# The down projection of two SwiGLU blocks in Strassen's seven block products

## The chip, the cores and the metric

The kernel runs on one core of a Trainium2 chip. The metric is the device time of one execution in microseconds (us). TensorE (PE) multiplies, VectorE (DVE) and ScalarE (ACT) work on tiles in the two on-chip memories SBUF and PSUM, GpSimd (POOL) works on SBUF tiles, and DMA queues bring weights from HBM; most transfers are issued by SyncE (SP).

## The reference

Two layers of a decoder trunk over 512 positions of width 1024, in float32. Each layer mixes tokens with four groups of heads, projects out, and then runs a SwiGLU block of inner width 2816:

```python
for l in range(DEPTH):                      # DEPTH = 2
    h = rms_norm(x, norm_mix_w[l])
    ...                                     # in projection, four token mixers
    x = x + y @ w_out[l]
    h = rms_norm(x, norm_ffn_w[l])
    x = x + (silu(h @ w_gate[l]) * (h @ w_up[l])) @ w_down[l]
return rms_norm(x, final_norm_w)
```

The change is in the last product of a layer, by `w_down` (2816 x 1024).

## The kernel before

**Layout.** Activations lie transposed: `x[0..7]` are eight tiles of 128 channels x 512 positions. The inner width 2816 makes KF = 22 tiles `j` of 128 rows ("hidden tiles"), the output width KD = 8 tiles `m`.

**Precision.** Every matmul operand is split into a high part (a copy to fp32r by ACT) and a low part (value minus high part, by DVE or POOL). `mm3` issues three matmuls for one 128x128 weight block: high x high, high x low, low x high (lines L429, L430, L431). The weights are split on the fly: `split_w` (L249, L250) for plain pieces, `s_item` (L341 to L359) for Strassen pieces.

**Order.** `items` is a list, written out ahead, of weight pieces in the order in which PE uses them. `w_next` takes the next one, splits one or more later ones ahead (up to AHEAD = 5 Strassen items) and lets SP load later pieces (L323). Split weights lie in four slots of the pool `wsp`, and within the SwiGLU part in four more of `ffw`. PSUM is two pools of four banks each, `pd` and `pm`. The framework orders the instructions of each engine by program order and a simulated time line, so that work that is ready may go ahead of work that is not.

**The SwiGLU part of a layer.** For the first five hidden tiles (`hidden_plain`, N_PLAIN = 5) gate and up are plain products: 8 blocks x 3 matmuls of 512 columns each. Meanwhile `operand(k)`, k = 0..3, prepares the seven Strassen operands of the normalised x: DVE and ACT build e, g, h, t1, t2, t3, t4 (each 256 columns wide; L1487 to L1495) in `bh`, `bl`. From tile 5 on, `hidden(j)` computes gate and up together as a 2x2 block product with seven block products instead of eight (`product`, 4 blocks x 3 matmuls of 256 columns each, so 84 matmuls a step). The two weight pieces of a step give seven items: a, b, d as they are, and s1, s2, s4 (sums made by DVE in a `pd` bank) and s3 (made by POOL). The seventh product and the multiplication of a step (L1556) are put off into the next step by `last` and `finish`. `leave_hidden` then splits the finished tile (ACT L1504, DVE L1505).

**The down projection** is plain, in two parts, because the split tiles don't all fit: `SPLIT_FF = [15, 7]` gives layer 0 a first part of 15 hidden tiles and a second of 7, layer 1 a first of 7 and a second of 15. `down(part)` runs for each `m` over the tiles of its part, 3 matmuls of 512 columns each, into a `pd` bank, and adds the sum to `x[m]` (L1587). In the second part of layer 0 `x[m]` is also split for the next layer and stored by SP (L1594). In the second part of layer 1 the last two `m` are done in two halves of 256 columns (`down_order`, TAIL = 2); within the second run of the first of these second halves `leave(0)` scales the finished first half (`rstd_spread`, DVE and POOL L1568 and L1566) and issues its stores from SP and ACT (L1569). `leave(1)` does the same for the second half at the end.

Of the kernel before, what the change touches and what calls it, by code (L numbers as in the profile page):

```python
# [16 lines left out]
P = 128  # L17
# [22 lines left out]
SPLIT_FF = [15, 7]  # L40
# [90 lines left out]
def kernel(  # L131
# [135 lines left out]
    def ff_parts(l):  # L267
        return [range(0, SPLIT_FF[l]), range(SPLIT_FF[l], KF)]

    def part_order(l, part):  # L270
        return down_order(l) if part else [(m, slice(0, T)) for m in range(KD)]

    def eights(ks, short=False):

        n = 4 if short else 0
        return [ks[:n]] * short + [ks[i:i + 8] for i in range(n, len(ks), 8)]

    for l in range(DEPTH):
        for nm in ORDER:
            if nm == "gg":  # L280
                for g in range(2):
                    plain(wg[l, g], 4 * (G + 2 * H))
            elif nm in T_GROUPS:
                for g in range(2):
                    plain(wt[l, 2 * T_GROUPS.index(nm) + g], 4 * G)
            else:
                plain(wc[l, C_TILES.index(nm)], KD * P)
        for m, g in OUT_ORDER:
            plain(wo[l, m][:, g * 4 * P:(g + 1) * 4 * P], 4 * P)
        left = None  # L290
        for part, js in enumerate(ff_parts(l)):
            for j in js:
                if j < N_PLAIN:
                    for q in range(2):
                        plain(wf[l, 2 * j + q], KD * P, V)
                    continue
                pj = len(pieces)
                pieces.extend((wf[l, 2 * j + q], KD * P) for q in range(2))
                for u in ("a", "s1", "d", "s2", "b", "s4", "s3"):
                    if u != "d":  # L300
                        items.append((u, pj))
                    elif left is not None:
                        items.append((u, left))
                left = pj
            for n_m, (m, _) in enumerate(part_order(l, part)):
                for n8, k8 in enumerate(eights(js, n_m == 0)):
                    plain(wd[l, m][:, k8[0] * P:(k8[-1] + 1) * P], len(k8) * P)
                    if n_m == n8 == 0 and left is not None:
                        items.append(("d", left))
                        left = None  # L310
# [1109 lines left out]
    for l in range(DEPTH):  # L1420
# [47 lines left out]
        with tc.tile_pool(name=f"ffp{l}", bufs=1, reuse_waits="tile") as ffp, \  # L1468
# [3 lines left out]
            own = [[ffp.tile([P, T], F32R, name=f"{q}{k}") for q in ("ph", "pl")] for k in range(KF - max(SPLIT_FF))]  # L1472
            both_h = own + [[xh[k], xl[k]] for k in range(KD)]
            hid = {j: both_h[n] for js in ff_parts(l) for n, j in enumerate(js)}

            HC = T // 2
            bh = [ffp.tile([P, 7 * HC], F32R, name=f"bh{k}") for k in range(KD // 2)]
            bl = [ffp.tile([P, 7 * HC], F32R, name=f"bl{k}") for k in range(KD // 2)]
            B_E, B_G, B_H, B_T1, B_T2, B_T3, B_T4 = (slice(n * HC, (n + 1) * HC) for n in range(7))

            def operand(k):
                ef, gh = fft.tile([P, T], F32, name="gs"), fft.tile([P, T], F32, name="sg")
                t12, t34 = pm.tile([P, T], F32, name="pm"), pm.tile([P, T], F32, name="pm")
                lo, up = slice(0, HC), slice(HC, T)
                for q, t in enumerate((ef, gh)):
                    kk = k + q * KD // 2
                    V.scalar_tensor_tensor(t, x[kk], col(o + V_NFFN + kk), rsb, op0=MUL, op1=MUL)  # L1487
                V.tensor_tensor(t12[:, lo], ef[:, up], ef[:, lo], op=SUB)
                V.tensor_tensor(t34[:, lo], ef[:, up], gh[:, up], op=ADD)
                V.tensor_tensor(t12[:, up], gh[:, up], t12[:, lo], op=ADD)  # L1490
                V.tensor_tensor(t34[:, up], gh[:, lo], t12[:, up], op=SUB)
                for t, c in ((ef[:, lo], B_E), (gh, slice(HC, 3 * HC)), (t12, slice(3 * HC, 5 * HC)),
                             (t34, slice(5 * HC, 7 * HC))):
                    S.copy(bh[k][:, c], t)  # L1494
                    V.tensor_tensor(bl[k][:, c], t, bh[k][:, c].bitcast(F32), op=SUB)  # L1495

            def product(ps, c, first=False):
                hi, lo = w_next()
                for k in range(KD // 2):
                    mm3(ps, hi, lo, k, bh[k][:, c], bl[k][:, c], first and k == 0, k == KD // 2 - 1, True)  # L1500

            def leave_hidden(j, v):
                hi, lo = hid[j]
                S.copy(hi, v)  # L1504
                V.tensor_tensor(lo, v, hi.bitcast(F32), op=SUB)  # L1505

            def hidden_plain(j):
# [7 lines left out]
                gs = fft.tile([P, T], F32, name="gs")  # L1515
                sg = fft.tile([P, T], F32, name="sg")
                V.tensor_tensor(gs, pg, rsb, op=MUL)
                S.activation(sg, gs, AF.Silu)
                V.tensor_tensor(sg, sg, rsb, op=MUL)
                V.tensor_tensor(gs, pu, sg, op=MUL)  # L1520
                leave_hidden(j, gs)
# [9 lines left out]
            def hidden(j):  # L1531
# [13 lines left out]
                S.copy(gs[:, up], cd[:, lo])
                product(ab[:, lo], B_G)
                product(ab[:, up], B_H)
                V.tensor_tensor(ab, ab, gs, op=ADD)
                S.activation(sg, ab, AF.Silu)
                product(cd[:, lo], B_T3)  # L1550
                S.copy(u3, cd[:, lo])
                V.tensor_tensor(cd[:, up], cd[:, up], u3, op=ADD)

                def end():
                    product(cd[:, lo], B_T4)
                    V.tensor_tensor(cd, cd, sg, op=MUL)  # L1556
                    leave_hidden(j, cd)
                last.append(end)

# [11 lines left out]
            def down(part):  # L1571
                js = ff_parts(l)[part]
                order = part_order(l, part)
                for n_m, (m, c) in enumerate(order):
                    ps = pd.tile([P, T], F32, name="pd")[:, c]
                    for n8, k8 in enumerate(eights(js, n_m == 0)):
                        hv = w_next()
                        for n, k in enumerate(k8):
                            ph, pl = hid[k]
                            mm3(ps, *hv[n // 4], n % 4, ph[:, c], pl[:, c], k == js[0], k == js[-1])  # L1580
# [6 lines left out]
                    V.tensor_tensor(x[m][:, c], x[m][:, c], ps, op=ADD)  # L1587
                    if not part:
                        continue
# [8 lines left out]
                return sq if part and l + 1 == DEPTH else None  # L1598

            for part, js in enumerate(ff_parts(l)):  # L1600
                for j in js:
# [3 lines left out]
                sq = down(part)  # L1605
# [6 lines left out]
def pack(inputs):  # L1612
# [55 lines left out]
    wd = np.stack([np.stack([ctile(a["ffn_w_down"][l][:, m * P:(m + 1) * P]) for m in range(KD)])  # L1668
# [25 lines left out]
```

## Time and profile before

| what | value |
|---|---|
| median of 3 runs | 1355.92 us (1354.26 to 1356.53) |
| the profiled execution | 1356.95 us, its span 1355.1 us |
| PE busy, its weight loads busy | 1308.9 us (97%), 1166.0 us (86%) |
| DVE, ACT, POOL busy | 752.9 (56%), 647.9 (48%), 737.1 us (54%) |
| mean granted PE clock | 0.975 |
| HBM read and written | 117.61 and 6.82 MB |

The profile follows one execution. A line such as L1587 is a line of the kernel. In a row of a group, "out<-in" gives the tiles by name, then their shapes, the count, the busy time and the mean duration; what stands behind "idle before" is how long the engine had waited just before and for whom. [...] The two SwiGLU parts lie at about 328 to 681 us and 990 to 1344 us.

### The profile page before, as it was taken

The page shows a single profiled execution, that of the slowest core. Times are in us where ns is not written, and L with a number is a line of the kernel's source. Part 1 is how long each engine was busy: PE and PEld are TensorE (multiplying, and loading weights), DVE is VectorE, ACT ScalarE, POOL GpSimd, SP SyncE. Part 2 cuts the span into 40 slices and gives each one's busy share as a digit, 9 for nine tenths or more (in the row PEclk, how much of TensorE's full clock was granted, in tenths as well). Part 3 has the DMA queues.
Part 4 walks back from the last instruction along what each step waited for, and adds up shares of the span by engine and source line. Part 5 has one row for each costly group of instructions (what it writes and reads, how often), then busy time and mean ns, then how long its engine had stood idle before and what let it go on. Part 6 is the DMA issues. An engine that isn't in the chain of part 4 may idle for free.

```text
span 1355.1 us, 22065 instructions
## 1 busy us (share of the span) xinstructions
PE 1308.9 (97%) x8402; PEld 1166.0 (86%) x8402; DVE 752.9 (56%) x1305; ACT 647.9 (48%) x1276; POOL 737.1 (54%) x627
## 2 busy tenths in 40 slices
PE   8899988999999999999999999999999999999997
PEld 6788987988889988899888887888887889999887
DVE  4653769637886620255456367777569336655113
ACT  5453454535556632365445345445444436666333
POOL 5376674933046644565545766747602366666444
PEclk8899989989999999999999999989999999999998
DMA  6223210134223333233432222002422333233333
GB/s 245 66 77 105 65 48 9 48 93 129 89 84 110 109 99 101 91 100 111 149 110 94 80 80 73 23 5 75 142 92 85 88 104 113 96 109 113 95 96 112
DMA packets 58506, 125.85 MB, mean 93 GB/s; under 512 B 17312, under 2 KB 24736, under 8 KB 58400
## 3 DMA queue, kind: packets, MB, share of 16 engines
q1 hardware_dynamic: 56960, 123.27, 28.9%
q8 instruction: 66, 1.08, 0.3%
q10 hardware_dynamic: 1440, 1.18, 0.3%
q14 instruction: 40, 0.33, 0.1%
HBM read 117.61 MB, written 6.82 MB: 92 GB/s over the span
## 4 chain that ended last, share of the span: by engine, by line
PE 86%; DVE 7%; POOL 3%; ACT 1%; issue 1%; DMA 1%; POOLq 0%; SPq 0%; DVEq 0%; ACTq 0%
PE pd L429 15%; PE pd L430 15%; PE pd L431 15%; PE pm L429 8%; PE pm L430 8%; PE pm L431 8%; PE pd L459 2%; PE pd L458 2%; PE pd L457 2%; PE pm L1126 2%; POOL wlo L250 1%; DVE x L1229 1%; PE pm L865 1%; POOL ar L718 0%; PE pm L1019 0%
## 5 line engine op out<-in xcount | busy, mean ns | idle before, releaser
L250 POOL TENSOR_TENSOR wlo<-wraw,whi 128x512 fp32r<-128x512 f32 (+1 forms) x240 | 309.1, 1295 | 260.5 <-ACT whi L249 258.9
L249 ACT CAST whi<-wraw 128x512 fp32r<-128x512 f32 (+2 forms) x288 | 173.5, 606 | 329.0 <-PE pd L430 232.1
L430 PE MATMUL pm<-bl,whi 128*128 128x256 f32 x952 | 267.5, 282 | 3.5 <-DVE bl L1495 3.5
L429 PE MATMUL pm<-bh,whi 128*128 128x256 f32 x952 | 267.4, 283 | 1.8 <-ACT bh L1494 1.0
L359 POOL TENSOR_TENSOR wlo<-wraw,whi 128x512 fp32r<-128x512 f32 x136 | 179.0, 1328 | 158.6 <-ACT whi L358 142.2
L431 PE MATMUL pm<-bh,wlo 128*128 128x256 f32 x952 | 265.0, 281 | 0.0
L429 PE MATMUL pd<-xh,whi 128*128 128x512 f32 (+1 forms) x592 | 232.6, 394 | 4.8 <-DVE pm L914 2.3
L430 PE MATMUL pd<-xl,whi 128*128 128x512 f32 (+1 forms) x592 | 231.6, 392 | 1.0 <-DVE xl L244 1.0
L431 PE MATMUL pd<-xh,wlo 128*128 128x512 f32 (+1 forms) x592 | 231.2, 392 | 0.0
L430 PEld LDWEIGHTS pm<-bl,whi 128*128 128x128 f32 x952 | 181.1, 190 | 4.4 <-DVE bl L1495 3.9
L429 PEld LDWEIGHTS pm<-bh,whi 128*128 128x128 f32 x952 | 180.7, 190 | 4.5 <-PE pd L431 1.6
L431 PEld LDWEIGHTS pm<-bh,wlo 128*128 128x128 f32 x952 | 180.0, 190 | 0.1
L429 PEld LDWEIGHTS pd<-xh,whi 128*128 128x128 f32 x592 | 112.7, 190 | 29.5 <-ACT ar L1029 2.4
L430 PEld LDWEIGHTS pd<-xl,whi 128*128 128x128 f32 x592 | 112.5, 190 | 25.7 <-DVE xl L244 2.8
L431 PEld LDWEIGHTS pd<-xh,wlo 128*128 128x128 f32 x592 | 112.7, 190 | 24.0
L358 ACT CAST whi<-wraw 128x512 fp32r<-128x512 f32 x136 | 84.5, 622 | 53.3 <-PE pm L430 29.1
L457 PE MATMUL pd<-whi,xh 128*128 128x256 f32 (+1 forms) x320 | 93.5, 294 | 5.5 <-DVE ar L562 4.4
L458 PE MATMUL pd<-wlo,xh 128*128 128x256 f32 (+1 forms) x320 | 93.8, 294 | 0.0
L459 PE MATMUL pd<-whi,xl 128*128 128x256 f32 (+1 forms) x320 | 93.2, 293 | 0.0
L430 PE MATMUL pd<-pl,whi 128*128 128x512 f32 (+1 forms) x238 | 90.4, 381 | 0.0
L429 PE MATMUL pd<-ph,whi 128*128 128x512 f32 (+1 forms) x238 | 90.3, 382 | 0.0
L1587 DVE TENSOR_TENSOR x<-x,pd 128x512 f32<-128x512 f32 (+1 forms) x34 | 22.0, 655 | 123.0 <-PE pd L431 123.0
(317 smaller groups left out, 2521.2 us busy)
## 6 DMA issues: line engine op xcount, KB each, us to landing
wraw<-in_wf_dram SPq DMA_DIRECT2D x88, 512.0 KB, 3.5
wraw<-in_wc_dram SPq DMA_DIRECT2D x35, 512.0 KB, 3.5
wraw<-in_wd_dram SPq DMA_DIRECT2D x30, 448.0 KB, 3.3
wraw<-in_wd_dram SPq DMA_DIRECT2D x18, 512.0 KB, 3.6
wraw<-in_wt_dram SPq DMA_DIRECT2D x16, 512.0 KB, 3.5
wraw<-in_wo_dram SPq DMA_DIRECT2D x32, 256.0 KB, 2.6
x<-in_xt_dram SPq DMA_DIRECT2D x16, 256.0 KB, 4.3
wraw<-in_wg_dram SPq DMA_DIRECT2D x4, 528.0 KB, 3.6
```

The costliest lines, as they stand in the source:

```text
L249: S.copy(hi[:, :n], r)
L250: eng.tensor_tensor(lo[:, :n], r, hi[:, :n].bitcast(F32), op=SUB)
L358: S.copy(hi, src)
L359: eng.tensor_tensor(lo, src, hi.bitcast(F32), op=SUB)
L429: PE.matmul(ps, hi[:, w], ah, start=first, stop=False, skip_group_check=shared)
L430: PE.matmul(ps, hi[:, w], al, start=False, stop=False, skip_group_check=shared)
L431: PE.matmul(ps, lo[:, w], ah, start=False, stop=last, skip_group_check=shared)
L457: PE.matmul(o, xh[k][:, tk], hi[:, w], start=(k == 0 and b % per == 0), stop=False)
L458: PE.matmul(o, xh[k][:, tk], lo[:, w], start=False, stop=False)
L459: PE.matmul(o, xl[k][:, tk], hi[:, w], start=False, stop=(k == KD - 1 and b % per == per - 1))
L1126: PE.matmul(ps[:, (bb * 2 + ct) * P:(bb * 2 + ct + 1) * P], k[:, ct * T + b * P:ct * T + (b + 1) * P], qx[:, (ct * NB + b) * P:(ct * NB + ...
L1587: V.tensor_tensor(x[m][:, c], x[m][:, c], ps, op=ADD)
```

## The change

The down projection of hidden tiles 0 to 7 (part 0) and 8 to 15 (part 1) is also done by Strassen's seven products, two output tiles `m = 2q, 2q+1` at a time, so four steps of 84 matmuls a part; tiles 16 to 21 (`rest`) stay plain. Part 0 runs after hidden tile 8, part 1 after hidden tile 16. The body of `hidden(j)` becomes `step(of, first, second)`, used by both. A finished hidden tile is no longer split as it is: it goes to a `sqp` tile, and the seven operands of a pair of tiles are built by `blocks_even` and `blocks_odd` in banks of `pm` (tiles below 5) or `pd`. The same two functions replace the body of `operand`. `leave(0)` moves from within item (6, second half) to after the matmuls of (7, second half). The rows of `w_down` are packed in another order.

```diff
+PART = 8
+N_PARTS = KF // PART
...
+    steps = []
+    for j in range(KF):
+        steps.append(("hidden", j))
+        if j and j % PART == 0:
+            steps += [("down", j // PART - 1, q) for q in range(KD // 2)]
+    steps.append(("rest",))
+    rest = range(PART * N_PARTS, KF)
...
+                two = [wd[l, m][:, part * PART * P:(part + 1) * PART * P] for m in (2 * q, 2 * q + 1)]
...
-                late = i >= len(items) - 4 * TAIL
+                late = i >= len(items) - 2 * TAIL
...
+            own = [ffp.tile([P, T], F32R, name=f"ph{k}") for k in range(2 * 7)]
+            seven = own + xh + xl
+            seven = [seven[7 * k:7 * k + 7] for k in range(PART // 2)]
+            hid = {j: own[2 * n:2 * n + 2] for n, j in enumerate(rest)}
...
+            def split(v, hi, lo):
+                S.copy(hi, v)
+                V.tensor_tensor(lo, v, hi.bitcast(F32), op=SUB)
...
+            def blocks_even(pool, ef, of):
+                t1 = bank(pool)
+                V.tensor_tensor(t1[:, LO], ef[:, UP], ef[:, LO], op=SUB)
+                split(ef[:, LO], *of("e"))
+                split(t1[:, LO], *of("t1"))
+
+            def blocks_odd(pool, ef, gh, of, gh_, t23_):
+                t23, t4 = bank(pool), bank(pool)
+                V.tensor_tensor(t23[:, UP], ef[:, UP], gh[:, UP], op=ADD)
+                V.tensor_tensor(t23[:, LO], t23[:, UP], ef[:, LO], op=SUB)
+                V.tensor_tensor(t4[:, LO], gh[:, LO], t23[:, LO], op=SUB)
+                split(gh, *gh_)
+                split(t23, *t23_)
+                split(t4[:, LO], *of("t4"))
...
+            def hidden_split(j):
+                if j in rest:
+                    split(raw.pop(j), *hid[j])
+                    return
+                pool, k = pm if j < N_PLAIN else pd, j % PART // 2
+                if j % 2 == 0:
+                    blocks_even(pool, raw[j], lambda nm: of_hidden(k, nm))
+                else:
+                    blocks_odd(pool, raw.pop(j - 1), raw.pop(j), lambda nm: of_hidden(k, nm), seven[k][3:5], seven[k][5:7])
...
+                def up(cd):
+                    if j in rest and j != rest[0]:
+                        raw[j] = cd
+                        V.tensor_tensor(cd, cd, sg, op=MUL)
+                        hidden_split(j)
+                    else:
+                        raw[j] = sqp.tile([P, T], F32, name="sq")
+                        V.tensor_tensor(raw[j], cd, sg, op=MUL)
+                        if j % PART or j == 0:
+                            hidden_split(j)
+                step(of_x, lambda ab: S.activation(sg, ab, AF.Silu), up)
+
+            def down(part, q):
+                def add(m):
+                    return lambda ps: V.tensor_tensor(x[m], x[m], ps, op=ADD)
+                step(of_hidden, add(2 * q), add(2 * q + 1))
+                if q == KD // 2 - 1:
+                    last.append(lambda: hidden_split(PART * (part + 1)))
...
-                        if part and l + 1 == DEPTH and n_m == KD:
-                            if n8 == 0:
-                                rstd_sum(range(NB // 2), ssq)
-                            else:
-                                leave(0)
+                    if l + 1 == DEPTH and n_m == KD:
+                        rstd_sum(range(NB // 2), ssq)
+                    if l + 1 == DEPTH and n_m == KD + 1:
+                        leave(0)
                     V.tensor_tensor(x[m][:, c], x[m][:, c], ps, op=ADD)
```

More of the change, by code (lines that the diff above doesn't have):

```diff
@@ L39 @@
 N_PLAIN = 5
-SPLIT_FF = [15, 7]
+PART = 8
+N_PARTS = KF // PART
+DOWN_K = [PART * p + k for p in range(N_PARTS) for k in (*range(0, PART, 2), *range(1, PART, 2))] + list(
+    range(PART * N_PARTS, KF))
 AHEAD = 5
@@ L265, in plain, with runs @@
         pieces.append((ap, n))
[L267 to L276, printed above, removed]
+    steps = []
[5 more added lines that the diff above has]
+    rest = range(PART * N_PARTS, KF)
+    def runs(short=False):
+        return [rest[:4], rest[4:]] if short else [rest]
     for l in range(DEPTH):
@@ L290 @@
         left = None
[L291 to L295, printed above, removed]
-                    continue
[L297 to L310, printed above, removed]
+        for what, *n in steps:
+            if what == "rest":
+                for n_m, (m, _) in enumerate(down_order(l)):
+                    for r in runs(n_m == 0):
+                        plain(wd[l, m][:, r[0] * P:(r[-1] + 1) * P], len(r) * P)
+                        if left is not None:
+                            items.append(("d", left))
+                            left = None
+                continue
+            if what == "hidden":
+                two = [wf[l, 2 * n[0] + q] for q in range(2)]
+                if n[0] < N_PLAIN:
+                    for ap in two:
+                        plain(ap, KD * P, V)
+                    continue
+            else:
+                part, q = n
+                two = [wd[l, m][:, part * PART * P:(part + 1) * PART * P] for m in (2 * q, 2 * q + 1)]
+            pj = len(pieces)
+            pieces.extend((ap, KD * P) for ap in two)
+            for u in ("a", "s1", "d", "s2", "b", "s4", "s3"):
+                if u != "d":
+                    items.append((u, pj))
+                elif left is not None:
+                    items.append((u, left))
+            left = pj
     raws, halves, sums = {}, {}, {}
@@ L1497, in product @@
[L1497 to L1505, printed above, removed]
+                    if q == 0:
+                        blocks_even(pm, t, lambda nm: of_x(k, nm))
+                blocks_odd(pm, *two, lambda nm: of_x(k, nm), *([t[:, n * HC:(n + 2) * HC] for t in bx[k]] for n in (1, 4)))
@@ L1529, in finish, with step, product @@
                 last.clear()
-            def hidden(j):
+            def step(of, first, second):
+                def product(ps, nm, start=False):
+                    hi, lo = w_next()
+                    for k in range(KD // 2):
+                        mm3(ps, hi, lo, k, *of(k, nm), start and k == 0, k == KD // 2 - 1, True)
                 ab = pm.tile([P, T], F32, name="pm")
@@ L1546, in hidden @@
[L1546 to L1557, printed above, removed]
@@ new lines, in step, with end, hidden @@
+                first(ab)
+                product(cd[:, LO], "t3")
+                S.copy(u3, cd[:, LO])
+                V.tensor_tensor(cd[:, UP], cd[:, UP], u3, op=ADD)
+                def end():
+                    product(cd[:, LO], "t4")
+                    second(cd)
+                last.append(end)
+            def hidden(j):
+                sg = fft.tile([P, T], F32, name="sg")
+                def up(cd):
[3 more added lines that the diff above has]
+                        hidden_split(j)
+                    else:
+                        raw[j] = sqp.tile([P, T], F32, name="sq")
+                        V.tensor_tensor(raw[j], cd, sg, op=MUL)
+                        if j % PART or j == 0:
+                            hidden_split(j)
+                step(of_x, lambda ab: S.activation(sg, ab, AF.Silu), up)
@@ L1604 @@
                         operand(j)
-                sq = down(part)
+                elif what == "down":
+                    down(*n)
+                else:
+                    sq = down_rest()
             extra.clear()
```

87 lines of the change are left out of this document (42 added, 45 removed).

## The prediction

> **What bounds the kernel now.** I read the page's busy shares first, then its chain of waits, then the stages by windows.
>
> ```profile
> PE 1308.9 (97%) x8402; PEld 1166.0 (86%) x8402; DVE 752.9 (56%) x1305; ACT 647.9 (48%) x1276; POOL 737.1 (54%) x627
> PE 86%; DVE 7%; POOL 3%; ACT 1%; issue 1%; DMA 1%; POOLq 0%; SPq 0%; DVEq 0%; ACTq 0%
> ```
>
> PE is busy 97% of the span and holds 86% of the chain, so fewer or shorter matmuls pay where PE stays fed. What a matmul costs is its pace, read in stretches bounded by an instruction that comes once a step (L1556) or once an output tile (L1587).
>
> ```profile
> core 0: us, PE busy (x) PEld busy (x) DVE busy (x) ACT busy (x) POOL busy (x), PEclk, DMA share, GB/s
> 1143.10:1252.90 109.80, 109.76 (x928) 109.16 (x927) 66.42 (x108) 69.06 (x142) 71.11 (x55) 1.00 0.33 107
> 412.88:482.22 69.34, 69.34 (x588) 69.03 (x588) 42.99 (x69) 43.73 (x91) 44.99 (x35) 1.00 0.32 100
> 596.09:635.32 39.23, 39.23 (x333) 39.04 (x332) 23.41 (x39) 24.97 (x52) 26.28 (x22) 1.00 0.30 95
> L1556 DVE TENSOR_TENSOR pm<-pm,sg x12: 699/700/700, 1143.1 to 1252.9; 128x512 f32<-128x512 f32 x12
> L1587 DVE TENSOR_TENSOR x<-x,pd x7: 686/689/689, 509.8 to 572.5; 128x512 f32<-128x512 f32 x7
> L1587 DVE TENSOR_TENSOR x<-x,pd x4: 686/688/689, 1280.3 to 1311.6; 128x512 f32<-128x512 f32 x4
> 1321.78:1343.99 22.21, 22.21 (x189) 1.00 0.29 87
> ```
>
> The first three windows hold 11, 7 and 4 Strassen steps (12 L1556 bound 11), together 218.4 us for 22 steps: 9.92 us a step, 0.1181 us for each of 84 matmuls of 256 columns. Plain: 6 output tiles of 45 matmuls in 62.7 us are 0.2324 us each in layer 0, 3 in 31.3 us are 0.2313 us in layer 1. The plain half-width tail takes 22.2 us for 180 matmuls and 8 tiny ones; allowing some 0.7 us for those, 0.119 us. PE is never idle there: PE busy equals the window.
>
> [...]
>
> **The matmuls.** Layer 0 loses 384 plain ones (16 tiles x 8 x 3) and gains 672 (8 steps x 84): 89.2 - 79.4 = 9.8 us. Layer 1 loses 330 of full width (438 become 108) and 108 of half width (180 become 72, as the halved tail runs over 6 tiles instead of 15), and gains 672: 76.3 + 12.9 - 79.4 = 9.8 us. Sum **-19.6 us**.
>
> **VectorE in the steps.** A finished pair of tiles costs 7 operations of 256 columns and 2 of 512 instead of 2 of 512.
>
> ```profile
> L1505 DVE TENSOR_TENSOR pl<-pm,ph 128x512 fp32r<-128x512 f32 x7 | 4.8, 690 | 2.9 <-ACT ph L1504 2.9
> L1552 DVE TENSOR_TENSOR pm<-pm,u 128x256 f32<-128x256 f32 x15 | 6.4, 429 | 6.8 <-ACT u L1551 6.8
> L341 DVE TENSOR_TENSOR pd<-wraw 128x512 f32<-128x512 f32 x13 | 10.3, 790 | 10.9 <-DMA wraw<-in_wf_dram 10.9
> L345 DVE TENSOR_TENSOR pd<-wraw,pd 128x512 f32<-128x512 f32 x14 | 9.6, 685 | 0.0
> L359 POOL TENSOR_TENSOR wlo<-wraw,whi 128x512 fp32r<-128x512 f32 x56 | 72.8, 1313 | 33.2 <-ACT whi L358 29.9 <-PE pm L430 1.9 <-PE pm L431 0.4
> L1545 ACT COPY gs<-pm 128x256 f32<-128x256 f32 x15 | 5.6, 375 | 0.0
> L1504 ACT CAST ph<-pm 128x512 fp32r<-128x512 f32 x7 | 4.1, 588 | 4.7 <-DVE pm L1556 4.7
> ```
>
> With 0.43 and 0.69 us that is +0.6 us for an even tile, +2.4 for an odd one (3 + 1 of 256, 2 of 512, less one). DVE has 66.42/11 = 6.0 us in a step of 9.9, so 6.6 and 8.4. ACT rises from 6.3 by at most 1.0 (copies of 0.59 + 0.59 + 0.38 less 0.59); POOL stays at 6.5. Down steps have DVE at 6.0 too (two additions to `x` for the multiplication and the split). All fit in 9.9, so on average the cover holds, but an odd step leaves DVE 1.5 us. I take 1 us in all for late operands in the 22 steps with tiles 5 to 15; bounds 0 (today PE doesn't wait) and 8.
>
> How the upper bound comes: four new operations of a pair have both inputs in SBUF. L341 has that form and takes 0.79 us where L345, with one input in PSUM, takes 0.69. The worst that such an operation shows is this row, beside POOL's work:
>
> ```profile
> 385.75 1.79 DVE L1505 TENSOR_TENSOR pl<-gs,ph 128x512 fp32r<-128x512 f32 x1
> ```
>
> That is 1.1 us over the 0.69. With two of those an odd step takes DVE 10.6 us, 0.7 too long: 8 us over the 12 odd steps (5 to 15, two layers) if even steps (8.8) take up none of it. [...]
>
> **VectorE between plain tiles and Strassen steps.** This is the one place where DVE is the bound already.
>
> ```profile
> 344.88:393.83 48.95, 46.30 (x211) 38.26 (x210) 48.52 (x80) 26.87 (x50) 12.75 (x8) 0.97 0.23 76
> 387.46 0.42 DVE L1491 TENSOR_TENSOR pm<-sg,pm 128x256 f32<-128x256 f32 x1
> 387.79 1.44 DVE L1519 TENSOR_TENSOR sg<-sg,rsb 128x512 f32<-128x512 f32 x1
> 389.33 0.69 DVE L1520 TENSOR_TENSOR gs<-pd,sg 128x512 f32<-128x512 f32 x1
> 389.94 1.28 DVE L1495 TENSOR_TENSOR bl<-pm,bh 128x512 fp32r<-128x512 f32 x2
> 388.55 0.39 PE L429 MATMUL pm<-bh,whi 128*128 128x256 f32 x1 [0.46 <-ACT bh L1494]
> 390.68 0.58 PE L430 MATMUL pm<-bl,whi 128*128 128x256 f32 x1 [1.74 <-DVE bl L1495]
> 393.62 0.41 PE L431 MATMUL pm<-bh,wlo 128*128 128x256 f32 x1
> 393.83 0.34 PE L429 MATMUL pm<-bh,whi 128*128 128x256 f32 x1
> 1052.47 0.38 PE L430 MATMUL pm<-bl,whi 128*128 128x256 f32 x1 [1.74 <-DVE bl L1495]
> ```
>
> DVE works 48.5 of 48.95 us, and PE waits 0.46 + 1.74 us for the last operand of x. Then its matmuls start 0.21 us apart for some 3 us instead of 0.118: another 1.3 us, at a granted clock of 0.97 in the stretch. So 3.5 us a layer are lost today (layer 1 shows the same 1.74). Back to back, a DVE operation costs 0.33 us (387.46 to 387.79) or 0.61 (389.33 to 389.94). Splitting tiles 0 to 3 adds 7 of 0.33 for each pair, 4.7 us for both, ahead of the last operand. Against it, `blocks_even` delivers e and t1 before anything else, where today t1 shares a copy with t2; the 24 matmuls of e and t1 and those of t2, g and h on k = 0..2 give some 3 us before PE needs the rest. What is late next is then t2 of k = 3. Bounds a layer: -3.5 (the wait goes) to +4.7 (all of it shows). `operand` now holds three `pm` banks instead of two, and the tile splits one or two of the same four, so I stay above the middle (+0.6): **+1.5 us a layer, +3 in all**.
>
> **The end.** Today `leave(0)` hides beside matmuls of (7, second half):
>
> ```profile
> 1340.36 0.39 PE L234 MATMUL pm<-cs,rst 128*128 128x128 f32 x2
> 1341.41 1.75 DVE L1568 TENSOR_TENSOR x<-x,pm 128x256 f32<-128x256 f32 x5 [1.11 <-ACT rsb L238]
> 1341.46 2.14 POOL L1566 TENSOR_TENSOR x<-x,rsb 128x256 f32<-128x256 f32 x3 [1.44 <-ACT rsb L238]
> 1341.87 1.90 ACTq L1569 DMA_DIRECT2D out_dram<-x  x4
> 1343.88 0.28 PE L431 MATMUL pd<-xh,wlo 128*128 128x256 f32 x1
> 1344.65 0.42 ACT L213 ACTIVATE sq<-x 128x256 f32<-128x256 f32 x1 [3.26 <-DVE x L1587]
> 1346.00 0.70 POOL L205 TENSOR_TENSOR rst<-ms,mhalf 128x2 f32<-128x2 f32 x1 [2.40 <-DVE ms L227]
> ```
>
> Moved behind the last matmul it loses that cover (the item now lasts 18 x 0.119 = 2.1 us instead of 5.4). The last addition to x[7], its square and its statistics must pass `leave(0)` on DVE (1.75 us), on POOL ahead of the power L205 (2.14) and on ACT behind four store issues (1.90). If the addition goes first, only POOL's 2.1 us stand in the way; if all pass in sequence, about 4. The least is 0, with the work slipped into today's waits of 2.4 and 3.3 us. I take **+2**. On SP the four stores have nothing behind them that is late.
>
> **Without price.** The weights' bytes and the DMA share (0.3) stay about as they are; SP's stores of x in layer 0 stand ahead of loads as before, an output tile now lasting 18 x 0.2324 = 4.2 us instead of 4.9; four raw pieces cover it, and without them a load would show its 3.6 us:
>
> ```profile
> wraw<-in_wd_dram SPq DMA_DIRECT2D x18, 512.0 KB, 3.6
> ```
>
> Tile 7 is finished seven products (9.8 us) before down needs its odd operands, tiles 8 and 16 are put off until their places are free, and neither holds anything up. At the rest's start PE may wait for tile 21, 1 us at most, but can take the next output tile meanwhile.
>
> **Sum.** -19.6 + 1 + 3 + 2 = -13.6 us against the profiled execution's 1356.95, which lies 1.0 us above the median: 1343.4 there, **1342 us** as a median.
>
> **The rivals.**
> (a) VectorE sets the pace where it prepares operands: the hand-over shows its full +4.7 us twice and half of the 8 us in odd steps shows: -19.6 + 9.4 + 4 + 2 = -4, about 1352 us. For it: 48.5 of 48.95 us busy. Against: 60% in the steps.
> (b) The new operand order takes the wait away: -3.5 twice, nothing in the steps, 1 us at the end: -25.6, about 1330 us. Against: 4.7 us of added work in a full queue.
> (c) Slower: the `pd` banks. The chain s1, s2, s4 holds up to three of four, and an odd tile needs two more (t23, t4). If weights stand still in each of the 12 odd steps for the life of these banks, about 4 us (six DVE and three ACT operations), that is +48 - 19.6 + 5, about 1389 us; from 1.2 us a step on nothing is won. Against: weights run up to five items ahead, and DVE has 1.5 us spare.
> (d) The change doesn't do what it says, because half-width matmuls are not worth half: excluded by 0.118 against 0.232 us.
>
> **How the numbers follow.** A measurement of this kernel can tell about 0.2% (2.7 us) from no change. My forecast (gain 8 to 18 us) 0.62; gain 18 to 26 (b and towards it) 0.15; gain 1 to 8 (a) 0.15, a quarter of that within 0.2%; (c) 0.08, of which 0.01 stays within 0.2%. So faster 0.88, same 0.05, slower 0.07. The range 1333 to 1353 leaves out (b)'s far end, (a)'s and (c).
>
> **What would show it.** PE matmuls rise by 288 in layer 0 and 234 in layer 1, to 8924; down steps last 9.9 us; PE's wait near 388 us lies between 0 and 7 us; DVE's busy time rises to some 885 us (24 us a layer for the splits, 48 for eight down steps of 6.0, less 5 for additions); the last matmul is followed by 11 to 15 us. Wrong if PE idles in odd steps behind DVE or ACT, or if down steps run at another pace.

## The result, and the profile after

The changed kernel takes 1374.84 us (median; 1369.5 to 1377.2), the kernel before, on the same chip, 1355.09 us (1354.25 to 1356.53). The ratio is 1.0139 [1.0107, 1.0171]: 1.4% slower, where 1342 us was forecast. The profiled execution has a span of 1373.4 us.

Busy time and the chain of waits on the page of after:

```profile
PE 1305.0 (95%) x8924; PEld 1187.5 (86%) x8924; DVE 892.4 (65%) x1565; ACT 701.8 (51%) x1440; POOL 757.2 (55%) x643
PE 80%; DVE 9%; POOL 4%; ACT 2%; DMA 2%; issue 2%; POOLq 0%; SPq 0%; DVEq 0%; ACTq 0%
```

The counts are those forecast: 8924 matmuls, DVE busy for some 140 us more. But PE's busy time has hardly fallen (1308.9 to 1305.0), and its share of the chain went from 86% to 80%. Of those six points DVE took two, and POOL, ACT, DMA and issue one each.

The windows of the two SwiGLU parts (start; length, then busy time and instructions of PE, PEld, DVE, ACT, POOL; granted clock), from their first statistics matmul to the next layer's, and in layer 1 to the last product's matmul; before, then after:

```profile
336.06:688.28 352.22, 349.56 (x2210) 315.20 (x2209) 177.34 (x277) 170.41 (x334) 179.17 (x141) 1.00 0.33 105
997.76:1343.88 346.12, 343.52 (x2275) 314.29 (x2274) 175.98 (x285) 173.89 (x339) 173.16 (x138) 1.00 0.31 99
```

```profile
334.32:695.03 360.71, 346.21 (x2498) 325.59 (x2497) 246.54 (x409) 199.45 (x418) 188.47 (x149) 0.99 0.33 103
1006.80:1360.30 353.50, 339.46 (x2500) 321.85 (x2499) 242.12 (x407) 198.12 (x418) 181.25 (x142) 0.98 0.30 92
493.06:542.39 49.33, 49.33 (x420) 49.33 (x419) 40.09 (x68) 32.38 (x72) 30.91 (x25) 1.00 0.29 91
462.66:482.09 19.43, 19.43 (x165) 19.43 (x165) 12.82 (x20) 10.30 (x22) 13.78 (x12) 1.00 0.28 91
```

Both parts became longer, by 8.5 and 7.4 us, while PE's busy time in them fell by 3 to 4 us: PE idles 14 us in each, where it idled 2.6. The last two windows are undisturbed stretches of hidden steps and of down steps: 49.33/420 = 0.1175 and 19.43/165 = 0.1178 us a matmul, so 84 take 9.9 us. The new matmuls are as cheap as forecast; PE is not fed.

An account by the starts of PE's matmuls, since their rows overlap (in before one of 256 columns starts at 600.01 us and lasts 0.28 us, the next starts at 600.13): a "loss" is what an interval between two starts has over 0.462 ns for each column (by the 0.1181 us for 256 columns in before's steps), so it counts waits and the slow matmuls behind them (0.21 us apart behind the wait of 6.43 us in after). "Between plain tiles and Strassen steps" (the hand-over) is here the time from 8 to 63 us behind the first statistics matmul of the SwiGLU part.

| us | forecast | measured |
|---|---|---|
| matmuls | -19.6 | -19.6 by the pace above |
| between plain tiles and Strassen steps: loss 5.0, 5.0 before, 12.4, 12.1 after | +3 | +14.5 |
| in the steps behind it: loss 0.5, 1.2 before, 10.6, 11.8 after | +1 | +20.7 |
| the end: 11.2 before, 13.1 after | +2 | +1.9 |
| the two mixers (code untouched): -1.8, +2.3 | 0 | +0.5 |
| sum | -13.6 | +18.0 (spans: +18.3) |

Two terms failed. The waits of PE in after, first from 334 to 396 us, then the largest from 395 to 695 us (total us, times, longest):

```profile
PE pm L441 <- DVE bl L1509: 6.4, 1, 6.4
PE pd L441 <- DVE pd L357: 2.5, 1, 2.5
```

```profile
PE pm L441 <- DVE x L1624: 2.9, 4, 1.4
```

**Between plain tiles and steps.** DVE's and PE's rows of that stretch (start, duration; what ended the idle time before): L1534 makes an operand pair's normalised input, L1517 its t1.

```profile
345.06 0.75 DVE L1534 SCALAR_TENSOR_TENSOR gs<-x,vc,rsb 128x512 f32<-128x512 f32 x1
363.91 0.42 DVE L1517 TENSOR_TENSOR pm<-gs 128x256 f32<-128x256 f32 x1
369.90 1.46 DVE L1534 SCALAR_TENSOR_TENSOR gs<-x,vc,rsb 128x512 f32<-128x512 f32 x1
390.79 0.42 DVE L1517 TENSOR_TENSOR pm<-gs 128x256 f32<-128x256 f32 x1
393.87 0.55 PE L441 MATMUL pm<-bh,whi 128*128 128x256 f32 x1 [6.43 <-DVE bl L1509]
```

The input of operand 1 is ready at 345.06 + 0.75, its t1 starts 18 us later; for operand 3 it is 19 us, and PE's 6.43 us end behind the low part of that t1 (L1509, 393.32 us). The t1 writes a `pm` bank. DVE does not pause meanwhile (busy for 18.10 of the 18.10 us from 345.81 and for 19.43 of the 19.43 us from 371.36): the t1 stands late in its queue. Here is DVE's work (fourth number) from the statistics matmul of layer 0 to the end of the last operand, in before, after, E1, E2 and E3 (described below):

```profile
336.06:391.22 55.16, 52.51 (x245) 43.19 (x244) 48.67 (x83) 28.53 (x53) 12.48 (x8) 0.99 0.26 86
334.32:396.07 61.75, 52.86 (x231) 43.21 (x230) 55.37 (x103) 30.36 (x62) 11.20 (x8) 0.94 0.25 77
333.53:394.43 60.90, 55.34 (x247) 45.48 (x246) 54.84 (x105) 31.75 (x67) 11.51 (x8) 0.94 0.26 78
332.98:392.95 59.97, 51.53 (x231) 41.99 (x230) 53.26 (x95) 30.42 (x62) 23.13 (x16) 0.95 0.26 79
336.32:392.37 56.05, 52.41 (x247) 42.98 (x246) 48.48 (x82) 31.10 (x65) 29.23 (x26) 1.00 0.28 85
```

From before to after DVE has 20 operations and 6.7 us more, and the operand is done 6.6 us later.

**In the steps.** DVE, PE and SP where the first long wait for `x` ends, at 451 us:

```profile
449.38 0.70 DVE L353 TENSOR_TENSOR pd<-wraw 128x512 f32<-128x512 f32 x1 [1.14 <-DMA wraw<-in_wd_dram]
449.99 0.68 DVE L371 TENSOR_TENSOR wlo<-pd,whi 128x512 fp32r<-128x512 f32 x1
450.59 0.68 DVE L1624 TENSOR_TENSOR x<-x,pm 128x512 f32<-128x512 f32 x1
451.41 0.36 PE L441 MATMUL pm<-ph,whi 128*128 128x256 f32 x1 [1.16 <-DVE x L1624]
445.65 4.10 SPq L335 DMA_DIRECT2D wraw<-in_wd_dram  x2
```

DVE stands still for 1.14 us at the sum s1 (L353), whose weights SP asked for only at 445.65. Behind it in DVE's queue stands the addition to `x` (L1624), which frees the `pm` bank that PE's next product needs. PE waits 1.16 us. The other long wait for `x` has the same rows: DVE waits 1.44 us for a load up to 572.36, PE 1.44 us up to 574.39. The remaining two are below 0.2 us. The same late DMA is there before, and larger; DVE's waits for DMA, after (397 to 690 us) and before (400 to 680):

```profile
DVE pd L353 <- DMA wraw<-in_wf_dram: 6.9, 5, 2.1
DVE pd L353 <- DMA wraw<-in_wd_dram: 3.7, 4, 1.4
```

```profile
DVE pd L341 <- DMA wraw<-in_wf_dram: 18.8, 11, 4.6
```

Before, DVE waited 18.8 us and PE had no wait at all in that stretch: in a hidden step ScalarE's silu frees that bank. In a down step it is DVE itself.

### The profile page after: what moved, and what is told of

Same layout as the page of the kernel before. It is cut to its first block, busy times and chain, and to the rows that moved or that the text cites. A ratio compares the mean times of both kernels' runs of the same rounds, so it can differ in the third digit from the quotient of the medians.

```text
span 1373.4 us, 23538 instructions
## 1 busy us (share of the span) xinstructions
PE 1305.0 (95%) x8924; PEld 1187.5 (86%) x8924; DVE 892.4 (65%) x1565; ACT 701.8 (51%) x1440; POOL 757.2 (55%) x643
## 4 chain that ended last, share of the span: by engine, by line
PE 80%; DVE 9%; POOL 4%; ACT 2%; DMA 2%; issue 2%; POOLq 0%; SPq 0%; DVEq 0%; ACTq 0%
PE pm L441 11%; PE pm L442 11%; PE pm L443 11%; PE pd L441 11%; PE pd L442 10%; PE pd L443 10%; PE pd L471 2%; PE pd L470 2%; PE pd L469 2%; PE pm L1138 2%; DMA wraw<-in_wd_dram 1%; POOL wlo L254 1%; DVE x L1241 1%; PE pm L877 1%; POOL wlo L371 1%
## 5 line engine op out<-in xcount | busy, mean ns | idle before, releaser
L371 POOL TENSOR_TENSOR wlo<-wraw,whi 128x512 fp32r<-128x512 f32 x200 | 263.8, 1335 | 190.4 <-ACT whi L370 181.4
L254 POOL TENSOR_TENSOR wlo<-wraw,whi 128x512 fp32r<-128x512 f32 (+2 forms) x176 | 225.6, 1290 | 178.2 <-ACT whi L253 174.5
L441 PE MATMUL pm<-bh,whi 128*128 128x256 f32 x952 | 271.2, 286 | 17.4 <-DVE bl L1509 13.1
L253 ACT CAST whi<-wraw 128x512 fp32r<-128x512 f32 (+1 forms) x220 | 131.1, 601 | 228.0 <-PE pd L442 153.2
L441 PE MATMUL pd<-xh,whi 128*128 128x512 f32 x448 | 181.5, 406 | 8.2 <-DVE pd L357 4.4
L442 PE MATMUL pd<-xl,whi 128*128 128x512 f32 x448 | 180.0, 403 | 1.1 <-DVE xl L248 1.1
L443 PE MATMUL pd<-xh,wlo 128*128 128x512 f32 x448 | 179.4, 403 | 0.0
L370 ACT CAST whi<-wraw 128x512 fp32r<-128x512 f32 x200 | 123.0, 625 | 60.4 <-PE pm L442 49.9
L371 DVE TENSOR_TENSOR wlo<-pd,whi 128x512 fp32r<-128x512 f32 x150 | 103.0, 687 | 52.9 <-ACT whi L370 45.5
L370 ACT CAST whi<-pd 128x512 fp32r<-128x512 f32 x150 | 88.5, 590 | 77.0 <-PE pm L442 38.5
L365 POOL TENSOR_TENSOR wraw<-wraw 128x512 f32<-128x512 f32 x50 | 66.0, 1320 | 99.4 <-DVE pd L353 52.4
```

The source lines that it names most:

```text
L253: S.copy(hi[:, :n], r)
L254: eng.tensor_tensor(lo[:, :n], r, hi[:, :n].bitcast(F32), op=SUB)
L365: GP.tensor_tensor(src, c, a, op=SUB)
L370: S.copy(hi, src)
L371: eng.tensor_tensor(lo, src, hi.bitcast(F32), op=SUB)
L441: PE.matmul(ps, hi[:, w], ah, start=first, stop=False, skip_group_check=shared)
```

## The experiments

"Same chip" medians of the kernel before are 1352.67 (E1 to E4), 1352.57 (E5 to E8), 1353.69 (E9 to E11), 1354.40 (E12) and 1352.46 us (E13, E14). From E3 on the lines of the code behind the edit are shifted. The table gives each kernel's loss in us a layer (layer 0/1), as defined above.

| kernel | SwiGLU parts | loss, plain to steps | loss behind it | ratio to before |
|---|---|---|---|---|
| before | 352.2, 346.1 | 5.0/5.0 | 0.5/1.2 | 1 |
| after | 360.7, 353.5 | 12.4/12.1 | 10.6/11.8 | 1.0139 [1.0107, 1.0171] |
| E1 banks | 357.4, 350.8 | 9.2/10.0 | 10.8/11.3 | 1.0078 [1.0045, 1.0110] |
| E2 POOL weights | 358.6, 351.4 | 10.6/10.5 | 11.1/11.2 | 1.0112 [1.0084, 1.0139] |
| E3 POOL splits | 352.2, 344.9 | 4.4/3.9 | 11.1/11.2 | 1.0019 [0.9998, 1.0039] |
| E4 x by copy | 360.1, 353.3 | 12.3/12.1 | 10.1/11.6 | 1.0113 [1.0029, 1.0198] |
| E5 five raw | 353.2, 345.0 | 8.5/8.1 | 7.2/7.0 | 1.0023 [1.0011, 1.0036] |
| E6 ahead 7 | 353.9, 344.2 | 6.8/6.6 | 10.4/8.0 | 1.0007 [0.9985, 1.0029] |
| E7 one part | 353.1, 344.2 | 6.6/5.3 | 4.7/4.8 | 1.0000 [0.9984, 1.0017] |
| E8 double low | 355.9, 347.5 | 4.3/4.2 | 14.1/13.7 | 1.0082 [1.0065, 1.0100] |
| E9 spare raw | 348.8, 340.3 | 4.3/4.0 | 7.8/7.2 | 0.9949 [0.9930, 0.9969] |
| E10 all cures | 352.6, 346.5 | 8.0/8.5 | 7.8/8.9 | 1.0009 [0.9992, 1.0027] |
| E11 and copy | 353.6, 346.0 | 8.1/7.8 | 8.8/9.2 | 1.0042 [1.0025, 1.0059] |
| E12 best | 348.8, 341.1 | 4.3/4.0 | 7.8/8.0 | 0.9941 [0.9921, 0.9961] |
| E13 ahead 6 | 348.8, 340.9 | 4.3/4.0 | 7.1/7.1 | 0.9977 [0.9960, 0.9994] |
| E14 ahead 7 | 349.9, 340.5 | 6.9/5.1 | 6.0/6.0 | 0.9974 [0.9961, 0.9987] |

The mixers, which no kernel changes, take from 331.2 to 336.3 us (layer 0) and from 304.3 to 311.8 us (layer 1) in these 16 traces; the losses are the steadier measure.

**E1, E2, E3: banks or DVE's work between plain tiles and steps.** E1 builds the operand blocks of tiles 0 to 4 in SBUF instead of `pm` banks, by the same engines (and splits t3 and t2 one by one instead of together). E2 leaves the banks and gives POOL half of DVE's splits of the plain weights. E3 is E1 with the blocks' sums and low parts on POOL.

```diff
 E1 and E3, hidden_split
+                if j < N_PLAIN:
+                    E = V                      # E3: GP
...
+                    t1 = fft.tile([P, HC], F32, name="u3")
+                    E.tensor_tensor(t1, ef[:, UP], ef[:, LO], op=SUB)
...
 E2, w_split
-                    halves[i].append(split_w(..., V if late and a == 0 else eng))
+                    halves[i].append(split_w(..., V if late and a == 0 else GP if a else eng))
```

E1:

> The operand blocks of hidden tiles 0 to 4 are built in small SBUF tiles instead of pm banks, by the same engines; all else as in the changed kernel. Theory B (the four pm banks are too few at the hand-over from plain tiles to Strassen steps): PE's waits there, 8.9 us in layer 0 and 8.6 in layer 1, fall below 4 each, and the time falls by 8 to 12 us from some 1375. Theory W (VectorE's added work sets the end of the hand-over): the waits stay at 8 to 9 us and the time within 3 us of 1375.

E2:

> The changed kernel, with POOL instead of VectorE making the low part of every second half of the plain tiles' weights: 8 operations of 0.61 us, 4.9 us a layer, less for VectorE, banks as they are. Theory W: PE's waits at the hand-over fall by about 5 us a layer, the time to about 1365. Theory B: they stay at 8 to 9 us, the time at 1375.

E3:

> The blocks of hidden tiles 0 to 4 built and split by POOL and ScalarE in SBUF tiles: VectorE loses 8.1 us of work a layer in the hand-over, and the pm banks go back to the operand alone. Theories W and B alike: PE's waits there fall to 3 us a layer or less, the time by 10 to 15 us to about 1362. If the waits stay above 6 us a layer, it is neither but the new order of operand building.

Measured 1362.44, 1369.53 and 1354.82 us. PE's waits from 334 to 396 us in E1, E2 and E3:

```profile
PE pm L441 <- DVE bl L1509: 3.5, 2, 2.6
PE pd L441 <- DVE sg L1587: 2.1, 1, 2.1
```

```profile
PE pm L441 <- DVE bl L1509: 7.0, 1, 7.0
PE pd L441 <- ACT whi L370: 0.8, 1, 0.8
PE pd L441 <- DVE sg L1562: 0.7, 1, 0.7
```

```profile
PE pm L441 <- DVE bl L1509: 1.8, 1, 1.8
PE pd L441 <- DVE sq L1590: 1.0, 1, 1.0
PE pd L441 <- DVE sg L1587: 0.8, 1, 0.8
```

E1: DVE's work is nearly unchanged (54.84 us for 55.37), these banks are free, and the t1 of the last operand starts 46.7 us behind the layer's first statistics matmul, where it was 56.5 us in after and 44.8 in before:

```profile
380.25 0.42 DVE L1517 TENSOR_TENSOR pm<-gs 128x256 f32<-128x256 f32 x1
```

The waits fall from 8.9 to 5.6 us (layer 1: 8.6 to 6.8), the loss by 3.2 and 2.1 us: between the two expectations. So the banks had put that t1 late by some 10 us. They are not the whole of its 19 us: in E1 it still starts 14.7 us behind its input, which is made earlier there.

E2: the wait for the last operand is 7.0 us, no shorter, since the other wait ahead of it shrinks and PE arrives earlier; the loss falls by 1.8 and 1.6 us. The eight operations that it moves should take 4.9 us off DVE, but DVE's work falls by only 2.1 us (55.37 to 53.26), because others became longer. So E2 tests less relief than it was meant to, and E1 and E2 do not rank banks and work.

E3 has both: DVE works 48.48 us, as long as before, and the loss is below that of before. From E1 to E3, with the banks alike, DVE has 6.4 us less to do and the loss falls by 4.8 and 6.1 us. So banks and work both count, and E3 takes away the whole of the hand-over's cost: some 8 us a layer of the two kernels' difference. How the 8 us divide is not settled. Its steps lose what after's lose.

**E4: the addition to `x` through a copy by ACT.** The bank is then freed by ACT's copy instead of DVE's addition.

```diff
-                step(of_hidden, add(2 * q), add(2 * q + 1))
+                def first(ps):
+                    t = fft.tile([P, T], F32, name="sg")
+                    S.copy(t, ps)
+                    V.tensor_tensor(x[2 * q], x[2 * q], t, op=ADD)
+                step(of_hidden, first, add(2 * q + 1))
```

> The changed kernel, with ScalarE copying the finished first sum of each down step out of its pm bank, so that the addition to x on VectorE no longer holds the bank. Theory R (PE waits for this addition because it stands in VectorE's queue behind s1, which waits for its weights): PE's waits for the addition, 2.9 us in layer 0 and 2.7 in layer 1, vanish and the time falls by 4 to 7 us to about 1369. Rival (weights are late in any case): the waits come back at other places of the same steps and the time stays within 2 us of 1375.

Measured 1369.15 us, with an interval too wide to tell it from after; that this is the time which theory R named proves nothing, since the kernel before was 2.4 us faster on this chip too. The loss in the steps stayed (10.1, 11.6), and PE's largest row of waits behind the hand-over is now for another DVE operation, the addition of L1600 to the same step's other bank:

```profile
PE pm L441 <- DVE pm L1600: 4.1, 4, 1.2
462.15 1.64 DVE L1628 TENSOR_TENSOR x<-x,sg 128x512 f32<-128x512 f32 x1
```

The second row shows a side effect. The addition to `x` now has both inputs in SBUF and takes 1.46 us in the median of 16, where it took 0.69 with one in PSUM; at 464.19 PE waits 1.13 us for L1600 behind it, without any wait of DVE for a load just ahead. So E4 made DVE's queue longer while it freed the bank earlier, and does not test the late load by itself. E5 and E9 do.

**E5, E6: on E3, a fifth raw piece, or seven items ahead.** E5 has five places for raw weights, and pays with one place for split ones; E6 sets AHEAD = 7.

```diff
 E5
-    wraw = ctx.enter_context(tc.tile_pool(name="wraw", bufs=4))
+    wraw = ctx.enter_context(tc.tile_pool(name="wraw", bufs=5))
...
-                tc.tile_pool(name=f"ffw{l}", bufs=4, reuse_waits="tile") as ffw, \
+                tc.tile_pool(name=f"ffw{l}", bufs=3, reuse_waits="tile") as ffw, \
 E6
-AHEAD = 5
+AHEAD = 7
```

E5:

> E3's kernel with five raw weight pieces instead of four (and seven split slots instead of eight in the SwiGLU part), so that weights are asked for one piece earlier. Theory R2 (in the steps PE waits because VectorE's queue stands behind s1, which waits for its weights' DMA): VectorE's waits for the DMA go, and PE's waits and slow matmuls behind the hand-over, 11 us in each layer in E3, fall below 5; the time falls by 8 to 12 us from some 1355. Rival S (the order of the queues, fixed ahead, puts operand splits before weights that PE needs first): no less than 9 us stay, the time within 3 us of 1355; one split slot fewer may even cost.

E6:

> E3's kernel with AHEAD = 7 instead of 5: up to seven Strassen items may be split ahead of PE. Rival S: weights stand further ahead in the queues than operand splits, so PE's waits on weight copies by ScalarE (1.8 us a layer) go, and 3 to 6 us of the 11 us a layer. Theory R2: no change, since the loads come no earlier; within 2 us of 1355.

Measured 1355.02 and 1354.37 us. In E5 DVE waits for no DMA at all from 397 to 690 us, PE's waits for `x` fall to 0.2 us, and the loss in the steps falls from 11 to 7. The missing split place brought a wait of 3.6 us for the weights' high part where the steps begin, and the loss there doubled. E6 shows no clear change in time: what its steps lose less (8.0 instead of 11.2 us in layer 1) is mostly lost again between plain tiles and steps.

**E7, E8: less and more of the change.** E7 does part 0 in plain form and only part 1 by Strassen's products, on after. E8 is E3 with each low part of blocks of tiles 5 and later made twice by DVE (12.6 us more of DVE's work a layer).

```diff
 E7
-        if j and j % PART == 0:
-            steps += [("down", j // PART - 1, q) for q in range(KD // 2)]
+        if j == PART - 1:
+            steps.append(("plain0",))
+        if j == 2 * PART:
+            steps += [("down", 1, q) for q in range(KD // 2)]
 E8, split
                 V.tensor_tensor(lo, v, hi.bitcast(F32), op=SUB)
+                if twice:
+                    V.tensor_tensor(lo, v, hi.bitcast(F32), op=SUB)
```

E7:

> The change in one part only: down by tiles 0 to 7 plain after hidden tile 7, by tiles 8 to 15 in Strassen steps, by 16 to 21 plain. Half of the matmul gain is left, 4.9 us a layer. If the costs sit in the splits of the plain tiles and at the boundary of each part: the wait at the hand-over falls to that of before (3 us a layer) and half of the 10 us in the later steps stays: SwiGLU parts about as long as before (352 and 346 us), the time 1354 to 1360. If the costs come from all Strassen steps alike, they stay near 10 us and the time is above 1362.

E8:

> E3's kernel in which VectorE makes each low part of the blocks of tiles 5 to 15 twice, 12.6 us more of its work a layer in the steps. Theory D (VectorE's amount of work in the steps is what PE waits for): the time rises by at least 5 us a layer, above 1365. Theory R2 or S (single operations that stand behind others in a queue): below 4 us in both layers together, 1355 to 1359.

Measured 1354.83 and 1363.49 us. E7: the loss in the steps is 4.7, less than half of after's, and the loss ahead of them is near that of before, since its early tiles need no blocks; half of the matmuls' gain is then just spent. E8: 12.6 us more of work cost some 3 us of loss a layer, between the two expectations. The amount of DVE's work matters, but a quarter of it shows.

**E9: a fifth raw piece at no split place's cost.** On E3, the place is a part of the constants that the mixers use and the SwiGLU part doesn't; it is loaded again after layer 0.

```diff
+            elif pos[0] in spare_ok and not any(isinstance(r, Pair) for r in raws.values()):
+                r = Pair(*(cs[:, C_COS + q * 512:C_COS + (q + 1) * 512] for q in range(2)))
+                nc.sync.dma_start(cs[:, C_COS:C_COS + 1024], ap)
...
+            if l + 1 < DEPTH:
+                nc.sync.dma_start(cs[:, C_COS:C_COS + 1024], cst[:, C_COS:C_COS + 1024])
```

> E3's kernel with a fifth place for a raw Strassen piece, in a stretch of the constants tile that the SwiGLU parts don't read (reloaded by one transfer of 512 KB after layer 0), and all eight split slots kept. Theory R2: PE's losses behind the hand-over fall from 11 us a layer to about 7 as in E5, with the hand-over as in E3 (4 us): the time falls by 7 to 9 us from some 1354.8. Rival (E5's gain there came from starting the steps later, behind its longer hand-over): they stay at 10 us and the time within 3 us of 1354.8.

Measured 1346.63 us: the first version that is faster than before. PE's waits from 330 to 700 us:

```profile
PE pm L457 <- ACT whi L386: 1.8, 1, 1.8
PE pm L457 <- DVE bl L1525: 1.8, 1, 1.8
...
PE pm L457 <- DVE x L1665: 0.2, 1, 0.2
```

DVE has no wait for DMA left, and the wait for the addition to `x` (now L1665) is 0.2 us. That is the test of the late DMA: with the piece asked for earlier the wait two steps down the queue is gone.

**E10, E11: more cures at once.** E10 is E9 with E2's edit and with `leave(0)` put off until just before `leave(1)`; E11 adds E4's edit.

```diff
-                    if l + 1 == DEPTH and n_m == KD + 1:
-                        leave(0)
...
                 rstd_sum(range(NB // 2, NB), ssq, sq)
+                leave(0)
                 leave(1)
```

E10:

> E9's kernel, with POOL making the low part of every second half of the plain tiles' weights, and with leave(0) issued after the statistics of the last half instead of ahead of the last addition. If R2 holds and each cure adds up: hand-over 2 to 4 us a layer, 7 us in the steps, the end back from 13.1 to about 11 us: some 1340 to 1344, faster than before by 0.7 to 1.0%. If VectorE's queue simply passes each wait on to the next place, 1350 or more.

E11:

> E10's kernel with ScalarE copying the first sum of a down step out of its bank, as in E4. If the wait of PE for additions to x behind s1 is gone with the fifth raw piece, this changes nothing (within 2 us of E10); if it is still there, another 2 to 4 us are won.

Measured 1354.42 and 1358.75 us: worse than E9. PE's longest waits in E10 from 330 to 700 us:

```profile
PE pm L457 <- ACT whi L386: 4.2, 2, 2.5
PE pd L457 <- ACT bh L1524: 2.5, 1, 2.5
```

PE now waits for copies by ACT, of weights and of an operand, and the loss between plain tiles and steps doubles to 8. So E2's edit, which gained a little on after, costs 10 us in the SwiGLU parts here (699.1 against 689.1 in E9). Why these copies come late is not shown: POOL, to which the work went, is busy for 38.96 of the first 60 us. E4's copy gains nothing: the SwiGLU parts take 699.6 us in E11, and what else separates E11 from E10 lies in the mixers of the two traces. The move of `leave(0)` paid: the last matmul is followed by 11.7 us instead of 13.1.

**E12: E9 with the move of `leave(0)` only.**

> E9's kernel with leave(0) issued after the statistics of the last half. E10 showed the end at 11.7 us with this against 13.1 us in E9; the SwiGLU parts should stay as in E9 (349 and 340 us): 1 to 2 us faster than E9's 1346.6, so about 1345, faster than before by 0.5 to 0.7%. If moving leave(0) reorders more than the end, the time stays within 1 us of E9 or rises.

Measured 1345.90 us, 0.59% faster than before: the two SwiGLU parts take 689.9 us together where before took 698.3, and the end 11.7. Of the 19.6 us of the matmuls some 8 arrive.

**E13, E14: what is left.** In E12 as in E1, E2, E3 and E9 PE waits 1.77 us, to the hundredth, at the start of the third step. E12's rows there, on DVE, POOL and PE:

```profile
402.98 0.69 DVE L1658 TENSOR_TENSOR sq<-pm,sg 128x512 f32<-128x512 f32 x1 [3.89 <-PE pm L459]
406.11 0.69 DVE L369 TENSOR_TENSOR pd<-cs 128x512 f32<-128x512 f32 x1
406.88 1.26 POOL L381 TENSOR_TENSOR cs<-cs,wraw 128x512 f32<-128x512 f32 x1 [8.65 <-DVE pd L369]
408.02 0.38 PE L457 MATMUL pm<-bh,whi 128*128 128x256 f32 x1 [1.77 <-ACT whi L386]
```

The sum s1 (L369) stands behind a finished tile's product (L1658), which waits 3.89 us for PE; POOL waits 8.65 us for that sum. E13 sets AHEAD = 6, E14 AHEAD = 7, on E12, so that s1 is written out ahead of the product.

E13:

> E12 with AHEAD = 6 instead of 5. In E12 the largest wait left behind the hand-over is 1.77 us at 408 us for a high part of weights (ACT whi), followed by some 2 us of slow matmuls: about 3.9 of the layer's 7.8 us. Its rows on DVE: s1 of the third step starts at 406.11, although its raw pieces were loaded by 398, behind the product of hidden tile 5 (402.98, after 3.89 us of idling for PE), which stands ahead of it in DVE's queue because s1 is written out five items ahead, after that product. Theory Q (order in DVE's queue): six items ahead puts s1 ahead of the product; the wait goes, the loss behind the hand-over falls to 3.5 to 5 us a layer, the time 5 to 8 us below E12's: ratio 0.988 to 0.991. Rival R (the loss moves): the same amount of work is late somewhere else, as in E6, where a wait of 1.2 us for whi came at 424; loss 7 to 10 us, ratio 0.993 to 0.998.

E14:

> E12 with AHEAD = 7. Theory Q: the same as with 6, since s1 of the third step passes the product in both: loss behind the hand-over 3.5 to 5 us a layer, ratio 0.988 to 0.991; the first wait for whi behind 400 us is gone. Rival R: with seven items ahead all eight places for split weights are taken, so a copy waits for PE to leave a place, as in E6: loss 7 to 10 us, ratio 0.993 to 0.998, and above E13.

Measured 1349.49 and 1349.99 us. DVE's rows in E13:

```profile
396.72 1.04 DVE L369 TENSOR_TENSOR pd<-cs 128x512 f32<-128x512 f32 x1
405.73 0.69 DVE L1658 TENSOR_TENSOR sq<-pm,sg 128x512 f32<-128x512 f32 x1 [3.87 <-PE pm L459]
```

The sum starts 9 us earlier, and the wait of 1.77 us is gone; that place was read rightly. But E13 has four waits for ScalarE's silu of 0.8 us each instead, which E12 hasn't:

```profile
PE pm L457 <- ACT sg L1661: 3.2, 4, 0.8
```

The loss in the steps is 7.1 us a layer (6.0 in E14, with 2.8 more ahead of them in layer 0 and 1.1 in layer 1). The rival that the loss moves was right. The SwiGLU parts of E12, E13 and E14 take 689.9, 689.7 and 690.4 us. The times of the last two are longer, though their intervals touch E12's; in the profiled executions the difference lies in the mixers (333.2 + 306.6 us in E12, 336.0 + 309.9 in E13), which `AHEAD` does not reach, and why they differ is open. No version beats E12, and E9 can't be told from it.

## Why the prediction was wrong

**Right.** The matmuls (8924, at 0.1175 to 0.1178 us), the down steps of 9.9 us, DVE's busy time in all (892 for 885) and the end. PE's wait near 388 us, 6.43 us, lies inside the 0 to 7 that were named. POOL's rows of after's end:

```profile
1363.14 2.10 POOL L1636 TENSOR_TENSOR x<-x,rsb 128x256 f32<-128x256 f32 x3 [1.25 <-ACT rsb L242]
1365.19 0.70 POOL L209 TENSOR_TENSOR rst<-ms,mhalf 128x2 f32<-128x2 f32 x1
```

POOL's 2.10 us of `leave(0)` stand ahead of the last power (L209), as the term of +2 said; +1.9 was measured.

**Wrong first: "I take 1 us in all for late operands in the 22 steps", bounds 0 and 8.** 20.7 us were measured. The step added up DVE's time for each step (6 to 8.4 of 9.9 us) and asked whether it fits. It does: in the undisturbed hidden steps DVE is busy 40.09 of 49.33 us. What failed is "today PE doesn't wait" as a lower bound and as cover: DVE did wait, 18.8 us in a layer, for its weights, and only silu on ACT hid it. A down step puts the freeing of PE's bank on the engine that waits. Of loads of `w_down` the prediction said only, for the plain rest, "four raw pieces cover it, and without them a load would show its 3.6 us"; for the down steps they stood at nothing, because PE didn't wait, without asking who did. E5 and E9 show the late load for some 3.5 us a layer. Of the other 7 a layer E13 shows that one wait, 1.77 us and the slow matmuls behind it, has the same kind of cause, order in DVE's queue, but that its cure brings other waits; E8 shows that the amount of work has a share. How these divide the 7 us is open.

**Wrong second: the hand-over, "+1.5 us a layer", bounds -3.5 and +4.7.** +7.4 and +7.1 were measured. Two things failed. DVE's added work was counted as 14 operations, 4.7 us; the windows above show 20 more and 6.7 us. Left out were four low parts of the operands (20 where before had 16) and three operations for tile 4; one operation on weights is fewer. And "`operand` now holds three `pm` banks instead of two, and the tile splits one or two of the same four" was seen and priced at 0.9 us above the middle of the bounds, where E1 gives back 3.2 and 2.1 us a layer by the banks alone. "`blocks_even` delivers e and t1 before anything else", the credit of 3 us, failed with the banks: t1 of the last operand started 19 us behind its input, together with the other blocks. The upper bound was too low because it took the counted work as the only cost.

**The rivals.** (a) had the hand-over's direction, at 9.4 of 14.5 us, and the steps at 4 of 20.7. (c), slower by the `pd` banks, has the sign but not the mechanism: PE waits once a layer for a sum in a `pd` bank (2.5 and 1.9 us, in the hand-over), and not in the odd steps. (b) and (d) didn't happen.

## What to carry to other kernels

When work moves to an engine that has time to spare, look at what that engine waits for today and who else waits behind it: a wait that costs nothing while another engine frees the buffers can be paid in full when this engine does. Count buffers as well as busy time, and count work by its rows in the new place: banks alone gave back 3.2 and 2.1 us here, and eight operations moved away took 2.1 us off a busy engine, not 4.9. Cures on one queue don't add up; each must be tried on the version that already has the others.

## What the hardware showed

Behind some waits PE's matmuls are slow. The window behind the wait of 6.43 us in after:

```profile
393.87:399.34 5.47, 5.47 (x25) 5.47 (x26) 3.51 (x8) 2.18 (x6) 0.00 (x0) 0.50 0.00 0
```

The granted clock is half, and matmuls start 0.21 us apart. The length of the wait alone does not decide this. E12 has two waits of nearly the same length, 1.78 us up to 388.98 and 1.77 us up to 408.02, and only behind the second does the clock fall. All changes of the granted clock in E12's trace, as in those of before and after, lie whole multiples of 3.413 us apart. Cut on that grid, the windows around the two waits are:

```profile
384.52:387.93 3.41, 2.67 (x23) 2.48 (x22) 3.28 (x6) 1.59 (x4) 3.41 (x4) 1.00 0.03 13
387.93:391.35 3.42, 2.37 (x20) 2.37 (x21) 2.51 (x5) 2.78 (x8) 3.42 (x4) 1.00 0.02 5
405.00:408.41 3.41, 1.64 (x13) 1.34 (x11) 2.98 (x8) 2.36 (x7) 1.26 (x1) 1.00 0.00 0
408.41:411.83 3.42, 3.40 (x16) 3.30 (x16) 2.34 (x4) 2.46 (x7) 3.27 (x3) 0.50 0.31 61
```

The first wait is shared by two windows, in which PE is busy 2.67 and 2.37 us, and the clock stays at 1.00. The second lies in one, where PE is busy 1.64 us, and the next window runs at half the clock. So the second wait cost some 3.7 us and the first some 2. Even behind 2.78 us in E14 (up to 1053.84) the clock stayed at 1.00. Nor does PE's busy time in one window decide it alone: in after, 1.63 us in the window from 385.81 to 389.22 were followed by one at 1.00, in which PE stood still. No run here shows where the limit lies.

E3 moved work that reads SBUF to POOL. In the first 60 us of layer 0's SwiGLU part POOL's busy time rose from 11.2 to 33.2 us, and PE's waits fell from 8.9 to 3.6 all the same: here the move paid. In E2, which also gave POOL work of DVE's, DVE's work fell by 2.1 us instead of 4.9; in E4 an addition took 1.46 us with both inputs in SBUF instead of 0.69 with one in PSUM. Why DVE's operations became longer is not shown.
